# Hybrid encoder layer with a product-key expert layer: one comparison and one product for the one-hot matrices, 30 kept blocks, and weight loads tied to the rows

## Chip, core and metric

The kernel runs on one core of a Trainium2 chip. The metric is the time of one execution on the device, in microseconds (us); of several runs the median is taken. A change of the time below some 0.2% can't be told from none.

## What is computed

One layer of a hybrid encoder for 512 tokens of width 1024: attention and a recurrent unit side by side, then a product-key expert layer (PEER), then a gated input. The change lies in the expert layer, which has 16384 experts (128 x 128) of one neuron each; a token uses 16 of them for each of 8 heads, 128 in all:

```python
q = (xn @ wq).reshape(B, S, PEER_HEADS, 2, HALF_KEY)
s1 = jnp.einsum('bshd,kd->bshk', q[..., 0, :], keys1)
s2 = jnp.einsum('bshd,kd->bshk', q[..., 1, :], keys2)
v1, i1 = lax.top_k(s1, PEER_TOPK); v2, i2 = lax.top_k(s2, PEER_TOPK)
...
idx = jnp.take_along_axis(cand_idx, pos, axis=-1)      # i1 * 128 + i2 of the 16 best sums
g = jax.nn.softmax(sc, axis=-1)
...
ue = exp_u[ib]
logits = jnp.einsum('td,tkd->tk', xb, ue)
act = jax.nn.gelu(logits) * gb
ve = exp_v[ib]
out = jnp.einsum('tk,tkd->td', act, ve)
```

## The kernel before

Tokens lie in four tiles of 128. For the first three tiles the kernel does not gather experts: it multiplies all tokens with all experts and weights the result with a matrix that is zero where an expert was not chosen. For the fourth tile it gathers 128 rows of `u` and 128 rows of `v` from DRAM, one row of 1024 for each token at a time, 512 KB for each such gather (256 in all).

**First sweep**, the loop `for j in range(P)` near the end of `trunk`: 128 blocks of 128 experts. A block's row `r` (512 KB of `ut`) is loaded on SP's queue by `row_load` (line 648), split into a high part `rh` (ScalarE, line 90) and a low part `rl` (VectorE, line 92), and multiplied with the tokens in 24 matmuls of 384 columns (`u_mm`, lines 97 to 99, PSUM tile `psl`). ScalarE takes the gelu out of PSUM (line 661) into `lg`. `advance` keeps three rows ahead; `r`, `rh`, `rl` have three buffers each, `psl` two. Every split's last instruction is put in the list `pace`.

The result of a block (192 KB) is stored to DRAM (`ld<-lg`, ScalarE's queue) or, for the last KEEP = 26 blocks, kept on chip in tiles of ten blocks (`keep`), of which the third lies in a pool that `settle` opens.

Between the blocks three generators are advanced by shares; each yields a cost for each piece of work, and `Background.run(share)` advances it until the share is used:

- `top`: ranks the tokens of a tile (`topk`), tile 3 first, then 0, 1, 2. Share TOP_FIRST until tile 0 is ranked, then TOP_THEN.
- `make`: `build` for tiles 0, 1, 2. For eight tokens at a time, `hot` makes on VectorE the one-hot matrices of the two key numbers: two comparisons with a ramp (line 831) and two products of the second one with the high and the low half of the weight (line 836), each of 1024 halves; HOT_DVE = 4 sends all of them to VectorE. Sixteen small matmuls (line 856, `pg`) turn them into the weight matrix of each token, ScalarE copies it to `sg` (line 859), and every 16 tokens 1 MB goes to DRAM as `gd`. Three tiles make 48 groups of eight.
- `side`: the gathered rows of tile 3 (`rows`; line 927 for `u`, line 934 for `v`), cost 1.15 each.

When `make` is done, `settle` closes the build's pools, at block `built + REST` or when the third kept tile is due, and opens those of the second sweep. From then on the loop issues the first weights.

**Second sweep**: 128 blocks in the order that begins with block 96. `v_prep` loads `lg` (if it was not kept) and one eighth of the next chunk of weights (`weights`, line 995: 192 KB, pieces of 512 bytes, `gc<-gd`; a chunk is eight blocks, there are two buffers), multiplies them (`am`, line 1065) and splits the product into `ah` and `al`. Eighteen matmuls of 512 columns a block add up into six PSUM banks (`acc`). `side` goes on with BG_V = 1.2 a block; from block 60 on, for 16 blocks, `prepare` loads and splits the weights of the gate instead. After the last block the gathered rows that are left run beside the closing steps of the first three token tiles (`finish`); tile 3 closes last.

The program is put in order by a planner (a list scheduler with modelled costs) that may move an instruction ahead of others on its engine when its inputs are free. `add_manual_dep` gives it an order: the gathers and the rows of `side` are tied to `pace` in this way, the loads of `weights` are not. An edge of the kind Sync makes the engine wait for a semaphore.

Of the kernel before, what the change touches and what calls it, by code (L numbers as in the profile page):

```python
# [11 lines left out]
F32 = mybir.dt.float32  # L12
R = mybir.dt.float32r
BF = mybir.dt.bfloat16
HF = mybir.dt.float16
I32 = mybir.dt.int32
U32 = mybir.dt.uint32
AF = mybir.ActivationFunctionType
ALU = mybir.AluOpType
# [3 lines left out]
P = 128  # L23
# [13 lines left out]
TB = 16  # L37
GBUFS = 4

KEEP = 26  # L40
G_SCALE = 2.0 ** 14
RO_AT = [2, 1, 1, 1, 1, 1, 1, 0, 0, 1, 0, 0, 1, 0, 0, 1, 0, 0, 1, 1, 9]
TOP_FIRST, TOP_THEN, MAKE, SIDE_1, SIDE, BG_V, HOT_DVE, PREP, SIDE_2 = 2.2, 1.0, 0.5, 0.6, 1.2, 1.2, 4, 60, 2.1
MAKE_2, REST = 0.62, 3
LAST = 3
N_HOT = 13
# [14 lines left out]
def trunk(ctx, tc, x, xT, pT, pos, w_lru, w_qkv, w_out, w_q, keys, wab, w_gate, w_proj,  # L61
          vec, row, ut, u, v, out, dbg=None):
    nc = tc.nc
# [83 lines left out]
    with ExitStack() as st:  # L147
# [129 lines left out]
        for ct in range(8):  # L277
# [12 lines left out]
            if ct < 4:  # L290
# [9 lines left out]
                                     scale=col(C_CW + ct), bias=col(C_CB + ct))  # L300
# [6 lines left out]
                for da in range(4):  # L307
                    i = da * 4 + ct
# [86 lines left out]
        for blk in range(3):  # L395
            accs = []

            for t in range(NT):
                tag = ((), ("ro", "po"), ("tr", None, None, "tr"))[blk][t:t + 1]
# [28 lines left out]
            for t in range(NT):  # L428
# [5 lines left out]
                if blk == 1:  # L434
                    g = qk[:, t, :].rearrange("p (g d) -> p g d", d=64)
# [202 lines left out]
    gd = dram.tile([NTB, P, P * TB], F32, name="gd")  # L638
# [31 lines left out]
    iota2 = bp.tile([P, P, 2], HF, name="iota2")  # L670
# [133 lines left out]

    def build(t, f1, f2):

        cols = []
        for i, src in enumerate((f1, f2, qg[:, t, :])):
            pt = psb.tile([P, P], F32, tag="tr", name="ptt", bufs=2)
            nc.tensor.transpose(pt, src, ident)  # L810
            sT = bw.tile([P, P], HF, tag=f"sT{i}", name="sT", bufs=1)

            nc.scalar.activation(sT, pt, AF.Copy, scale=G_SCALE if i == 2 else 1.0)
            cols.append(sT)
        gw = bw.tile([P, 2, P], F32, tag="gw", name="gw", bufs=1)
        nc.scalar.copy(gw[:, 0, :], cols[2])
        nc.vector.scalar_tensor_tensor(gw[:, 1, :], pt, G_SCALE, gw[:, 0, :], op0=ALU.mult, op1=ALU.subtract)
        gl = bw.tile([P, P], HF, tag="gl", name="gl", bufs=1)
        nc.vector.tensor_copy(gl, gw[:, 1, :])
        cols.append(gl)  # L820

        S3 = [P, 4, P, 2]

        def along(c, t0):
            return cols[c][:, t0:t0 + 8].rearrange("p (g i) -> p g i", i=2)[:, :, None, :].to_broadcast(S3)

        def hot(t0):
            o1 = bw.tile(S3, HF, tag="o1", name="o1")
            m2 = bw.tile(S3, HF, tag="m2", name="m2")
            for c, o in enumerate((o1, m2)):  # L830
                nc.vector.tensor_tensor(o, iota2[:, None, :, :].to_broadcast(S3), along(c, t0), op=ALU.is_equal)
            o2 = []
            for part in range(2):
                o = m2 if part else bw.tile(S3, HF, tag="o2", name="o2")
                if t0 // 8 % 2 * 2 + part < HOT_DVE:
                    nc.vector.tensor_tensor(o, m2, along(2 + part, t0), op=ALU.mult)
                else:
                    for i in range(8):
                        nc.scalar.activation(o[:, i // 2, :, i % 2], m2[:, i // 2, :, i % 2], AF.Copy,
                                             scale=gw[:, part, t0 + i:t0 + i + 1])  # L840
                o2.append(o)
            return o1, o2

        o12 = hot(0)
        yield 1.0
        for t0 in range(0, P, 8):
            if t0 % TB == 0:
                sg = bw.tile([P, P, TB], F32, tag="sg", name="sg")
            o1, o2 = o12
            if t0 + 8 < P:  # L850
                o12 = hot(t0 + 8)
            for q in range(0, 8, 4):
                pg = pgp.tile([P, 4, P], F32, tag="pg", name="pg")
                for i in range(q, q + 4):
                    for part in range(2):
                        nc.tensor.matmul(pg[:, i - q, :], lhsT=o1[:, i // 2, :, i % 2], rhs=o2[part][:, i // 2, :, i % 2],  # L856
                                         start=part == 0, stop=part == 1)
                s0 = t0 % TB + q
                nc.scalar.copy(sg[:, :, s0:s0 + 4].rearrange("p j t -> p t j"), pg)  # L859
            if (t0 + 8) % TB == 0:  # L860
                nc.scalar.dma_start(gd[(t * P + t0) // TB], sg.rearrange("p j t -> p (j t)"))
            yield 1.0
# [21 lines left out]
    bw = e0.enter_context(tc.tile_pool(name="bw", bufs=2, side="right", reuse_waits="tile"))  # L884

    pace, after = [], []
# [97 lines left out]
    JC = 8  # L984
# [10 lines left out]
    def weights(c, part, vp):  # L995

        if part == 0:
            gcs.append(vp.tile([P, NTB, JC, TB], F32, tag="gc", name="gc"))
        b0, b1 = part * NTB // JC, (part + 1) * NTB // JC
        j = order[c * JC]  # L1000
        nc.sync.dma_start(gcs[-1][:, b0:b1], gd[b0:b1, :, j * TB:(j + JC) * TB].rearrange("b p (j t) -> p b j t", t=TB))

    def settle():

# [10 lines left out]
    vp, gcs, built, parts = None, [], None, list(range(JC))  # L1015
    for j in range(P):
# [7 lines left out]
        else:  # L1024
            if j == P - KEEP:
                top.run(1e9)
            i = j - (P - KEEP)
# [288 lines left out]
```

## Time and profile before

| | us |
|---|---|
| median of 3 runs (lowest, highest) | 1499.4 (1499.07, 1501.27) |
| the profiled execution, its own time | 1503.23 |
| its span, first to last instruction | 1501.4 |
| up to the first sweep | 247 |
| first sweep | 650 |
| second sweep | 541 |
| end | 64 |

The stages were cut at the first and last matmul of each sweep. Busy time is what an engine spent in instructions; matmuls overlap, so a busy TensorE need not be at its peak rate, and the spacing of the starts tells the rate. In a timeline a bracket gives the idle time before an instruction and what ended it. PE is TensorE, DVE VectorE, ACT ScalarE; SPq and ACTq are the DMA issues of SP and ScalarE.

### The profile page before, as it was taken

Reading aid. Unit: us, or ns where it says so; the run is one execution under the profiler, and the core shown is the slowest. Engines: PE = TensorE matmul, PEld = TensorE weight load, DVE = VectorE, ACT = ScalarE, POOL = GpSimd, SP = SyncE. Lnnn points to the kernel's source line nnn. Section 1 sums busy time; section 2 is a strip of 40 time slices with the busy share of each in tenths; the row PEclk is TensorE's granted clock in tenths of the full one; section 3 lists DMA queues with packets and bytes.
Section 4 is the critical chain, followed back from the end, with each engine's and each line's share of the span. In section 5 each row is a group of like instructions: output and inputs, shape, how many; then the busy total and the mean of one; then the engine's idle time right before and its main releaser. Section 6 shows DMA issues by size and latency. Waiting matters only on the chain.

```text
span 1501.4 us, 22147 instructions
## 1 busy us (share of the span) xinstructions
PE 1463.8 (97%) x7907; PEld 1291.9 (86%) x7907; DVE 1254.9 (84%) x2481; ACT 738.1 (49%) x1059; POOL 388.6 (26%) x320
## 2 busy tenths in 40 slices
PE   9999999999899999999999989999999999999996
PEld 6887678899899999999999988878887888888875
DVE  7686987789999999999978658878887478878895
ACT  7974754354555655565555423333333453333345
POOL 0000000011223373235433342232222014344450
PEclk9999999999999999999999999999999999999998
DMA  7223022156789898889989899899999789999961
GB/s 257 65 90 126 15 92 81 48 195 228 238 295 336 286 349 321 309 293 330 394 306 337 304 325 348 290 308 334 348 353 340 236 272 360 362 349 363 323 224 71
DMA packets 169199, 394.21 MB, mean 263 GB/s; under 512 B 15360, under 2 KB 90880, under 8 KB 166016
## 3 DMA queue, kind: packets, MB, share of 16 engines
q1 hardware_dynamic: 112336, 207.52, 41.1%
q0 software_dynamic: 38464, 140.00, 26.2%
q10 hardware_dynamic: 18288, 45.27, 7.8%
q8 instruction: 62, 1.02, 0.3%
q14 instruction: 49, 0.40, 0.1%
HBM read 345.41 MB, written 47.32 MB: 262 GB/s over the span
## 4 chain that ended last, share of the span: by engine, by line
PE 57%; DVE 19%; DMA 9%; issue 8%; ACT 5%; POOL 1%; SPq 0%; ACTq 0%; DVEq 0%; POOLq 0%
PE acc L99 8%; PE acc L97 8%; PE acc L98 8%; PE psl L97 6%; PE psl L99 6%; PE psl L98 6%; DVE rl L92 4%; DMA r<-in_v_dram 2%; DMA r<-in_ut_dram 2%; PE ps L97 2%; PE pg L856 2%; PE ps L99 2%; PE ps L98 2%; DVE rr L927 2%; DVE h L934 1%
## 5 line engine op out<-in xcount | busy, mean ns | idle before, releaser
L90 ACT ACTIVATE rh<-r 128x1024 fp32r<-128x1024 f32 x256 | 270.9, 1059 | 466.3 <-PE psl L98 172.2
L92 DVE TENSOR_TENSOR rl<-r,rh 128x1024 fp32r<-128x1024 f32 x256 | 312.4, 1221 | 106.9 <-ACT rh L90 105.6
L97 PE MATMUL psl<-x2h,rh 128*128 128x384 f32 x1024 | 348.1, 340 | 7.2 <-ACT keep L661 4.8
L99 PE MATMUL psl<-x2h,rl 128*128 128x384 f32 x1024 | 344.1, 336 | 3.6 <-DVE rl L92 3.6
L98 PE MATMUL psl<-x2l,rh 128*128 128x384 f32 x1024 | 343.6, 336 | 0.0
L99 PE MATMUL acc<-rh,al 128*128 128x512 f32 x768 | 299.5, 390 | 2.7 <-DVE al L92 2.7
L97 PE MATMUL acc<-rh,ah 128*128 128x512 f32 x768 | 299.2, 390 | 1.6 <-ACT ah L90 1.6
L98 PE MATMUL acc<-rl,ah 128*128 128x512 f32 x768 | 299.0, 389 | 0.7 <-DVE rl L92 0.7
L895 POOL DMA_INDIRECT rr<-in_u_dram,qidx x84 | 112.7, 1342 | 387.8 <-DVE rl L92 186.2
L97 PEld LDWEIGHTS psl<-x2h,rh 128*128 128x128 f32 x1024 | 192.9, 188 | 8.8 <-ACT keep L661 5.1
L99 PEld LDWEIGHTS psl<-x2h,rl 128*128 128x128 f32 x1024 | 192.9, 188 | 5.2 <-DVE rl L92 5.1
L98 PEld LDWEIGHTS psl<-x2l,rh 128*128 128x128 f32 x1024 | 193.2, 189 | 0.0
L895 POOL DMA_INDIRECT rr<-in_v_dram,qidxv x82 | 135.7, 1655 | 196.2 <-DVE rl L92 168.9
L99 PEld LDWEIGHTS acc<-rh,al 128*128 128x128 f32 x768 | 144.1, 188 | 35.3 <-DVE al L92 5.7
L97 PEld LDWEIGHTS acc<-rh,ah 128*128 128x128 f32 x768 | 144.2, 188 | 32.4 <-ACT ah L90 2.9
L98 PEld LDWEIGHTS acc<-rl,ah 128*128 128x128 f32 x768 | 144.1, 188 | 31.0 <-DVE rl L92 1.1
L934 DVE SCALAR_TENSOR_TENSOR h<-rr,qg,h 128x1024 f32<-128x1024 f32 x82 | 105.0, 1280 | 6.4 <-DMA rr<-in_v_dram,qidxv 6.4
L927 DVE CUSTOM_DVE_ANT_0 rr<-rr,xn 128x1024 f32<-128x1024 f32 x84 | 102.2, 1218 | 5.0 <-DMA rr<-in_u_dram,qidx 5.0
L859 ACT COPY sg<-pg 128x512 f32<-128x512 f32 x96 | 95.8, 1107 | 1.0 <-ACT sc L696 0.3
L895 POOL DMA_INDIRECT xn<-in_v_dram,qidxv x46 | 67.7, 1472 | 99.4 <-DVE rl L92 92.1
L895 POOL DMA_INDIRECT xn<-in_u_dram,qidx x44 | 61.0, 1387 | 121.7 <-DVE rl L92 103.9
L90 ACT ACTIVATE ah<-am 128x384 fp32r<-128x384 f32 x128 | 65.7, 514 | 53.1 <-PE acc L98 28.7
(342 smaller groups left out, 2274.1 us busy)
## 6 DMA issues: line engine op xcount, KB each, us to landing
r<-in_ut_dram SPq DMA_DIRECT2D x128, 512.0 KB
r<-in_v_dram SPq DMA_DIRECT2D x128, 512.0 KB
gd<-sg ACTq DMA_DIRECT2D x24, 1024.0 KB
gc<-gd SPq DMA_DIRECT2D x128, 192.0 KB
ld<-lg ACTq DMA_DIRECT2D x102, 192.0 KB
lg<-ld SPq DMA_DIRECT2D x102, 192.0 KB
w<-in_w_qkv_dram SPq DMA_DIRECT2D x12, 512.0 KB
w<-in_w_out_dram SPq DMA_DIRECT2D x8, 512.0 KB
```

The source lines that it names most:

```text
L90: nc.scalar.activation(hi, src, AF.Copy, scale=1.0 if scale is None else scale)
L92: return nc.vector.tensor_sub(lo, src, hi.bitcast(F32))
L97: nc.tensor.matmul(ps, lhsT=lh, rhs=rh, start=first, stop=False)
L98: nc.tensor.matmul(ps, lhsT=lh, rhs=rl, start=False, stop=False)
L99: nc.tensor.matmul(ps, lhsT=ll, rhs=rh, start=False, stop=last)
L856: nc.tensor.matmul(pg[:, i - q, :], lhsT=o1[:, i // 2, :, i % 2], rhs=o2[part][:, i // 2, :, i % 2], start=part == 0, stop=part == 1)
L859: nc.scalar.copy(sg[:, :, s0:s0 + 4].rearrange("p j t -> p t j"), pg)
L895: g = nc.gpsimd.indirect_dma_start(out=dst, out_offset=None, in_=table, in_offset=bass.IndirectOffsetOnAxis(ap=idx, axis=0))
L927: behind(nc.vector.tensor_tensor_reduce(rr, rr, xn[:, t, :], 1.0, 0.0, ALU.mult, ALU.add, act[:, k % 16:k % 16 + 1]))
L934: behind(nc.vector.scalar_tensor_tensor(h[:, t, :], rr, qg[:, t, k:k + 1], h[:, t, :], op0=ALU.mult, op1=ALU.add))
```

## The change

One-hot matrices: the two key numbers of a tile of tokens lie in one tile `nums_`, the two halves of the weight in one tile `wts_`, eight tokens together. `hot` makes one comparison of 2048 halves, which writes the first and the third plane of a tile `o` of three, and one product of 2048, which reads the third plane twice and writes the second and the third. The low half of the weight is written as half precision by the subtraction itself; a cast falls away. HOT_DVE and its ScalarE branch go.

Kept blocks: KEEP goes from 26 to 30, which fills the third kept tile. So the ranking must be over at block 98 and not 102, and the third kept tile, and with it `settle`, is due at block 118 and not 122.

Weights: every load of `weights` waits (Sync) for `pace[-3]`, the split of the row two behind the newest.

Shares: TOP_FIRST 2.2 to 1.9, MAKE 0.5 to 0.57, SIDE_1 (the share of `side` until tile 0 is ranked) 0.6 to 0.85.

```diff
--- before.py
+++ after.py
@@ -37,10 +37,10 @@
 TB = 16
 GBUFS = 4
 
-KEEP = 26
+KEEP = 30
 G_SCALE = 2.0 ** 14
 RO_AT = [2, 1, 1, 1, 1, 1, 1, 0, 0, 1, 0, 0, 1, 0, 0, 1, 0, 0, 1, 1, 9]
-TOP_FIRST, TOP_THEN, MAKE, SIDE_1, SIDE, BG_V, HOT_DVE, PREP, SIDE_2 = 2.2, 1.0, 0.5, 0.6, 1.2, 1.2, 4, 60, 2.1
+TOP_FIRST, TOP_THEN, MAKE, SIDE_1, SIDE, BG_V, PREP, SIDE_2 = 1.9, 1.0, 0.57, 0.85, 1.2, 1.2, 60, 2.1
 MAKE_2, REST = 0.62, 3
 LAST = 3
 N_HOT = 13
@@ -804,42 +804,35 @@
 
     def build(t, f1, f2):
 
-        cols = []
+
+        nums_ = bw.tile([P, P // 8, 2, 8], HF, tag="sT0", name="sT0", bufs=1)
+        wts_ = bw.tile([P, P // 8, 2, 8], HF, tag="sT1", name="sT1", bufs=1)
+
+        def eights(a):
+            return a.rearrange("p (a b) -> p a b", b=8)
+
         for i, src in enumerate((f1, f2, qg[:, t, :])):
             pt = psb.tile([P, P], F32, tag="tr", name="ptt", bufs=2)
             nc.tensor.transpose(pt, src, ident)
-            sT = bw.tile([P, P], HF, tag=f"sT{i}", name="sT", bufs=1)
-
-            nc.scalar.activation(sT, pt, AF.Copy, scale=G_SCALE if i == 2 else 1.0)
-            cols.append(sT)
-        gw = bw.tile([P, 2, P], F32, tag="gw", name="gw", bufs=1)
-        nc.scalar.copy(gw[:, 0, :], cols[2])
-        nc.vector.scalar_tensor_tensor(gw[:, 1, :], pt, G_SCALE, gw[:, 0, :], op0=ALU.mult, op1=ALU.subtract)
-        gl = bw.tile([P, P], HF, tag="gl", name="gl", bufs=1)
-        nc.vector.tensor_copy(gl, gw[:, 1, :])
-        cols.append(gl)
-
-        S3 = [P, 4, P, 2]
+
+            nc.scalar.activation(nums_[:, :, i, :] if i < 2 else wts_[:, :, 0, :], eights(pt), AF.Copy,
+                                 scale=G_SCALE if i == 2 else 1.0)
+        gw = bw.tile([P, P], F32, tag="gw", name="gw", bufs=1)
+        nc.scalar.copy(eights(gw), wts_[:, :, 0, :])
+        nc.vector.scalar_tensor_tensor(wts_[:, :, 1, :], eights(pt), G_SCALE, eights(gw), op0=ALU.mult, op1=ALU.subtract)
+
+        S3 = [P, 8, P, 2]
 
         def along(c, t0):
-            return cols[c][:, t0:t0 + 8].rearrange("p (g i) -> p g i", i=2)[:, :, None, :].to_broadcast(S3)
+            return c[:, t0 // 8].rearrange("p c (g i) -> p (c g) i", i=2)[:, :, None, :].to_broadcast(S3)
 
         def hot(t0):
-            o1 = bw.tile(S3, HF, tag="o1", name="o1")
-            m2 = bw.tile(S3, HF, tag="m2", name="m2")
-            for c, o in enumerate((o1, m2)):
-                nc.vector.tensor_tensor(o, iota2[:, None, :, :].to_broadcast(S3), along(c, t0), op=ALU.is_equal)
-            o2 = []
-            for part in range(2):
-                o = m2 if part else bw.tile(S3, HF, tag="o2", name="o2")
-                if t0 // 8 % 2 * 2 + part < HOT_DVE:
-                    nc.vector.tensor_tensor(o, m2, along(2 + part, t0), op=ALU.mult)
-                else:
-                    for i in range(8):
-                        nc.scalar.activation(o[:, i // 2, :, i % 2], m2[:, i // 2, :, i % 2], AF.Copy,
-                                             scale=gw[:, part, t0 + i:t0 + i + 1])
-                o2.append(o)
-            return o1, o2
+
+            o = bw.tile([P, 3, 4, P, 2], HF, tag="o", name="o")
+            five = [P, 2, 4, P, 2]
+            nc.vector.tensor_tensor(o[:, 0:3:2], iota2[:, None, None].to_broadcast(five), along(nums_, t0), op=ALU.is_equal)
+            nc.vector.tensor_tensor(o[:, 1:3], o[:, 2:3].to_broadcast(five), along(wts_, t0), op=ALU.mult)
+            return o[:, 0], (o[:, 1], o[:, 2])
 
         o12 = hot(0)
         yield 1.0
@@ -998,7 +991,10 @@
             gcs.append(vp.tile([P, NTB, JC, TB], F32, tag="gc", name="gc"))
         b0, b1 = part * NTB // JC, (part + 1) * NTB // JC
         j = order[c * JC]
-        nc.sync.dma_start(gcs[-1][:, b0:b1], gd[b0:b1, :, j * TB:(j + JC) * TB].rearrange("b p (j t) -> p b j t", t=TB))
+        ld_ = nc.sync.dma_start(gcs[-1][:, b0:b1], gd[b0:b1, :, j * TB:(j + JC) * TB].rearrange("b p (j t) -> p b j t", t=TB))
+
+        tc.add_manual_dep(ld_.ins, pace[-3].ins.name,
+                          mybir.DependencyInfo(mybir.DependencyClass.Sync, mybir.DependencyReason.DATA), reason="pace")
 
     def settle():
```

## Rows read from the trace of the kernel before

**Rows 1.** The page, part 1: busy time, share and instructions by engine.

```profile
PE 1463.8 (97%) x7907; PEld 1291.9 (86%) x7907; DVE 1254.9 (84%) x2481; ACT 738.1 (49%) x1059; POOL 388.6 (26%) x320
```

**Rows 2.** Table of stages: length, busy by engine, granted clock, DMA share, GB/s.

```profile
247.00:897.00 650.00, 638.86 (x4148) 622.12 (x4149) 578.49 (x1453) 326.65 (x439) 205.76 (x127) 0.99 0.81 284
897.00:1438.00 541.00, 535.98 (x2357) 440.35 (x2356) 432.79 (x578) 209.41 (x287) 163.16 (x131) 1.00 0.94 326
...
350.00:400.00 50.00, 46.32 (x265) 44.72 (x263) 49.62 (x196) 23.41 (x32) 7.72 (x6) 1.00 0.66 216
...
700.00:750.00 50.00, 49.73 (x339) 48.50 (x338) 46.54 (x62) 26.02 (x36) 19.06 (x14) 1.00 0.98 381
...
850.00:900.00 50.00, 45.24 (x244) 44.05 (x243) 32.73 (x41) 15.32 (x22) 22.38 (x16) 0.93 0.96 334
...
1300.00:1400.00 100.00, 100.00 (x443) 82.81 (x442) 84.52 (x116) 37.08 (x51) 42.17 (x27) 1.00 1.01 352
...
1000.00:1010.00 10.00, 8.49 (x36) 5.99 (x35) 5.43 (x8) 4.00 (x5) 1.64 (x2) 1.00 0.95 333
```

**Rows 3.** Timeline of TensorE (start, length, engine, line), second sweep.

```profile
1431.97 0.39 PE L99 MATMUL acc<-rh,al 128*128 128x512 f32 x1
1432.20 0.39 PE L97 MATMUL acc<-rh,ah 128*128 128x512 f32 x1
```

**Rows 4.** Timeline of ScalarE at the seam (idle before and its releaser in brackets).

```profile
861.30 0.47 ACT L661 ACTIVATE keep<-psl 128x384 f32<-128x384 f32 x1
...
865.46 0.47 ACT L661 ACTIVATE keep<-psl 128x384 f32<-128x384 f32 x1
...
880.38 1.06 ACT L90 ACTIVATE rh<-r 128x1024 fp32r<-128x1024 f32 x1 [9.02 <-DMA r<-in_ut_dram]
...
893.34 0.47 ACT L661 ACTIVATE keep<-psl 128x384 f32<-128x384 f32 x1
```

**Rows 5.** Timeline of SP's queue at the seam, runs of one kind merged.

```profile
845.42 1.13 SPq L1001 DMA_DIRECT2D gc<-gd  x2
...
861.46 7.95 SPq L1001 DMA_DIRECT2D gc<-gd  x5
```

**Rows 6.** Timeline of TensorE at the seam.

```profile
876.77 0.34 PE L99 MATMUL psl<-x2h,rl 128*128 128x384 f32 x1
881.87 0.69 PE L97 MATMUL psl<-x2h,rh 128*128 128x384 f32 x1 [4.76 <-ACT keep L661]
882.36 0.52 PE L98 MATMUL psl<-x2l,rh 128*128 128x384 f32 x1
882.68 0.52 PE L99 MATMUL psl<-x2h,rl 128*128 128x384 f32 x1
```

**Rows 7.** Timeline of SP's queue, second sweep.

```profile
990.57 7.77 SPq L1001 DMA_DIRECT2D gc<-gd  x4
```

**Rows 8.** Timeline of ScalarE, second sweep.

```profile
1001.81 1.06 ACT L90 ACTIVATE rh<-r 128x1024 fp32r<-128x1024 f32 x1 [5.42 <-DMA r<-in_v_dram]
```

**Rows 9.** Timeline of ScalarE, first sweep.

```profile
378.83 0.31 ACT L738 ACTIVATE qg<-qg 128x128 f32<-128x128 f32 x1 [3.55 <-DVE qg L737]
```

**Rows 10.** Timeline of VectorE at the end: first and last of 18 gathered rows.

```profile
1440.17 1.27 DVE L934 SCALAR_TENSOR_TENSOR h<-rr,qg,h 128x1024 f32<-128x1024 f32 x1
...
1470.58 1.28 DVE L934 SCALAR_TENSOR_TENSOR h<-xn,qg,h 128x1024 f32<-128x1024 f32 x1
```

**Rows 11.** Timeline of TensorE at the end.

```profile
1477.57 1.97 PE L1154 MATMUL turn<-ident,x 128*128 128x128 f32 x8 [2.99 <-DVE x L1148]
```

**Rows 12.** Comparisons of line 831: shortest/median/longest ns, first and last start.

```profile
L831 DVE TENSOR_TENSOR o<-iota,sT x48: 672/684/722, 401.4 to 830.4; 128x1024 f16<-128x1024 f16 x48
```

**Rows 13.** Timeline of VectorE, first sweep: three instructions back to back.

```profile
666.18 1.22 DVE L781 TENSOR_TENSOR xn<-xn,sp 128x2048 f16<-128x2048 f16 x1
667.31 0.68 DVE L836 TENSOR_TENSOR m<-m,gl 128x1024 f16<-128x1024 f16 x1
667.91 1.47 DVE L771 TENSOR_TENSOR xn<-xn 128x1024 f16<-128x1024 f16 x3
```

## The prediction, on record before the result

> **What bounds the kernel now.** I read the page first, then the table of stages, then the timelines of the places where TensorE was not busy. The page has TensorE busy 97% of the span [rows 1]. The table of stages [rows 2] says where the rest is: the first sweep (247 to 897 us) has 638.86 us busy of 650, the second (897 to 1438 us) 535.98 of 541. So most of the kernel runs at the matmul rate, which this change leaves alone: second-sweep matmuls start every 0.227 us [rows 3], 18 of them make a block of 4.09 us, and first-sweep blocks end every 4.16 us, 24 matmuls of 0.173 us [rows 4]. What can be won is idle or slowed time. It lies in four places.
>
> Place A, the seam between the sweeps. Up to 865.46 a block ended every 4.16 us; from there to 893.34, five blocks, it took 27.88 us instead of 20.8, so 7.1 us were lost. In between ScalarE waited 9.02 us for one row `r` from DRAM [rows 4]. SP's queue shows why: from 845.42 on it issued 16 weight loads `gc`, both chunk buffers, as fast as the queue took them, with the row loads between; five of them took 7.95 us to issue [rows 5]. TensorE started nothing from 876.77 to 881.87, and its granted clock, 1.00 elsewhere in the sweep's stages shown, is 0.93 over 850 to 900 us [rows 2]: a part of that stretch ran at the lower of its two levels (1.2 instead of 2.4 GHz), and matmuls behind the gap start 0.32 us apart instead of 0.173 [rows 6]. So some 4.8 us of the 7.1 are idle and the rest is slow clock.
>
> Place B, the second sweep. The same burst comes once in eight blocks. At 990.57 the last four of eight `gc` took 7.77 us to issue [rows 7], the next row load stood behind them, ScalarE waited 5.42 us for it [rows 8], and TensorE was busy 8.49 of the 10 us from 1000 on [rows 2]. Other idle of this sweep falls where ScalarE waits for the gate's weights, which the change does not touch.
>
> Place C, the first sweep apart from the seam. Of its 11.1 us idle some 4.8 are A, so 6.3 are left, 3.7 of them in 350 to 400 us, where VectorE is busy 49.62 of 50 us [rows 2]. ScalarE, in order, stands there behind a step of the top-k that waits 3.55 us for VectorE [rows 9], and the splits and results behind it come late.
>
> Place D, the end. The last 18 gathered rows run on VectorE after the second sweep, from 1440.17 to 1470.58 [rows 10]; TensorE waits 2.99 us for the last token tile's normed rows, at 1477.57 [rows 11].
>
> **The change part by part.** 1. Weights in step. Each `gc` load now waits for the row split two behind the newest. Behind it on SP stand the spilled-block loads `lg` and the next row load. That row load waits for the same split anyway, since `r` has three buffers; nothing that was free is held. What moves: chunk 0 goes out as two loads a block over four blocks, later chunks as one a block, instead of in bursts of eight or sixteen. A part is first used more than two blocks (8 us) after its load. A block at the seam then moves 512 KB of row, two loads of 192 KB and about one gathered row of 512 KB: 1.44 MB in 4.16 us, 347 GB/s. From 700 to 750 us the core moved 381 GB/s with TensorE busy 49.73 of 50 us [rows 2]. So I expect the 7.1 us to shrink to 1, a gain of 6.1 (bounds 3 and 7.1). In B I take back the 1.5 us idle behind the burst (bounds 0 and 2.5, the upper one if the later row waits ease as well).
>
> 2. One comparison, one product. For each group of eight tokens VectorE ran two comparisons and two products of 1024 halves, 0.684 us long, 48 of each [rows 12]; now it runs one of each with 2048. The like is the product of 2048 halves in the top-k. An instruction starts before the end recorded for its forerunner, so I count from start to start: 1.13 us for 2048 (666.18 to 667.31), 0.60 us for 1024 (667.31 to 667.91) [rows 13]. A group falls from 4 x 0.60 = 2.40 to 2 x 1.13 = 2.26 us, and 48 groups save 6.7 us of VectorE. The Trainium skill, VectorE: DVE Perf Modes, section "Side-by-side: where the cycles go for N=2048 bf16", gives every instruction some 150 cycles of fixed cost and 1224 ns to 2048 halves at two per cycle. The trace agrees on the duration (1.22 us), not on what one more instruction costs, which the starts put at 0.07 us (2 x 0.60 - 1.13). By the page's fixed cost 96 instructions saved would be an estimated 15 us, and the sum below would gain what place C still holds, some 4 us, giving 1484.
>
> The rest of the build is hidden: ScalarE writes the same three columns a tile, now strided, and has 323 of 650 us free [rows 2]; were it not hidden, nine writes of 0.3 us would be under 3 us. The comparison writes two separate planes. The trace has no operation with that pattern; its bounds are 1.13 us and, at the rate of the 32-bit splits of 1024 elements, which VectorE starts 1.13 us apart, 2 x 1.13 = 2.26 us. I take 1.13, since type, inner pair and repeat of the operands are as before.
>
> 3. Shares. I counted the costs that the generators yield against the shares. Before: token tile 3 is ranked at block 8, then 16 blocks at 0.6, 94 at 1.2, 3 at 2.1, 4 at 1.2 and 3 at 2.1 give 139.8, over 1.15 that is 122 gathered rows in the first sweep. The second takes 113 + 3, so 18 of 256 are left, the number the trace has at the end [rows 10]. After: 19 blocks at 0.85, 90 at 1.2, 4 at 1.2 and 6 at 2.1 give 141.6, so 124, and 16 are left. A row takes 1.2 us there: VectorE has 2.4 us less in D. The last turn waits for that chain, but also for ScalarE's steps, so I take 2.0 (bounds 0 and 2.4). In C two more rows eat 2.4 of the 6.7 us, and the top-k is thinner in the first 28 blocks (1.9 for 2.2). Of the 6.3 us idle I take 2.0 back (bounds -3 and 6.3: the order of the steps is made anew, and another step may come to stand in ScalarE's way; 3 is about what the wait for the top-k cost).
>
> 4. 30 blocks kept. Four stores and four loads of 192 KB go, 1.5 MB, at 326 GB/s [rows 2] 4.7 us of DMA time for which TensorE did not wait: 0. The closing of the build pools moves from block 121 to 118, so that it comes one block behind the last group, not five. The first result in the third kept tile, and the first weights, may have to wait for the last 1 MB store of `gd`. That result must leave PSUM within two blocks (8.3 us), which covers the store (3.2 us at 326 GB/s) and a queue ahead of it as long again; uncovered it costs what the idle of A cost, up to 4.8 us. I take 0.
>
> Sum: 6.1 + 1.5 + 2.0 + 2.0 = 11.6 us. The profiled execution has a span of 1501.4 us and a time of 1503.23; the median of the runs is 1499.4, so it ran 0.26% above it. The span would be 1489.8, the profiled time 1491.6, the median **1488 us**.
>
> **The rivals.** R1, the rate of the DMA engines binds, not the order. A full second-sweep block moves 512 + 192 + 192 KB and 1.04 gathered rows of 512 KB: 1.46 MB in 4.09 us, 358 GB/s. Spreading loads would then shift lateness without removing it; half of A (3.5) and D (2.0) come back: 1494. For it: even in the 10 us with the idle behind the burst the DMA share was 0.95. Against it: 1300 to 1400 us has 352 GB/s with TensorE busy 100 of 100 us, and 381 GB/s came earlier [rows 2]. The Trainium skill, DMA: Bandwidth & Descriptors, section Specifications, puts one core's share of HBM at about 358 GB/s, which would leave a full block no slack; the 381 GB/s do not bear that out as a bound.
>
> R2, the relief of VectorE pays in full: all of A (7.1), 2.5 of B, 6.3 of C and 2.4 of D return, 18.3 us: 1481. For it: VectorE is 99% full in 350 to 400 us. Against it: part of C is ScalarE's order behind top-k steps, and those remain.
>
> R3, slower: the two-plane comparison loses the rate of two per cycle. 48 x (2.26 - 1.13) = 54 us of VectorE fall on a sweep in which it is busy 578 of 650 us. If half of it shows, and A, B and D still return 9.6: 1499.4 - 9.6 + 27 = 1517. It decides once the comparison runs above some 1.5 us. Against it: operands of the same type with the same inner pair ran at 0.684 us for 1024.
>
> R4, nothing: the planner still lets weights out in a burst, for instance because the splits they wait for are early themselves, and the early closing costs what D gives: 1499.
>
> **How the numbers follow.** Forecast 0.53, R1 0.17, R2 0.17, R3 0.07, R4 0.06. About 0.2% (3 us) is what a measurement of this kernel can tell from no change. Faster: the forecast less its spoilt cases, R2 and most of R1, 0.82. Same: R4 and the weak end of R1, 0.10. Slower: R3 and a forecast spoilt by the order in C, 0.08. At best the bounds of the terms give 18.3 us (1481), at worst 3 + 0 - 3 + 0 = 0. The range reaches from just below R2 past R1 to the worst case of the terms: 1479 to 1499.
>
> **What would show it.** After the change: `gc` on SP in ones and twos between row loads; no wait of ScalarE of 5 us or more for `r` at the seam or near 1000 us; TensorE's clock at 1.00 from 850 to 900 us; 48 comparisons of about 1.22 us; 16 gathered rows after the second sweep. I am wrong if comparisons take near 2.3 us (R3), if row waits stay as long (R1, R4), or if new idle stands near the third kept tile (part 4).

## Result, and the profile of the kernel after

The changed kernel takes 1484.95 us, the median of seven runs (1482.28 to 1492.08), against 1500.8 us for the kernel before, measured beside it (seven runs, 1499.07 to 1506.64). The ratio is 0.9894, 95% interval 0.9875 to 0.9912: some 16 us, or 1.1%, faster. The forecast was 1488, the range 1479 to 1499.

The profiled execution took 1491.43 us with a span of 1489.7, so it lies 6.5 us above its own median. The same file was profiled a second time in the experiments (called `after2`: 1487.59 us, span 1485.8; median of six 1485.52). Both stand in the tables below. The page, part 1, of the kernel after, to be read against [rows 1]:

```profile
PE 1462.2 (98%) x7907; PEld 1294.2 (87%) x7907; DVE 1246.7 (84%) x2382; ACT 737.3 (49%) x1059; POOL 375.3 (25%) x320
```

VectorE has 99 instructions and 8.2 us less, TensorE the same 7907 matmuls. The table of stages of the kernel after, columns as in [rows 2]; line numbers of this kernel lie up to 7 from those of before (the gathers are line 888, the rows of `v` line 927, the loads of the weights line 994):

```profile
250.00:890.00 640.00, 634.75 (x4144) 619.88 (x4145) 571.31 (x1356) 326.42 (x438) 197.12 (x128) 1.00 0.81 284
890.00:1432.00 542.00, 538.24 (x2366) 443.50 (x2365) 434.49 (x579) 208.94 (x287) 161.41 (x132) 1.00 0.94 330
...
850.00:900.00 50.00, 49.55 (x272) 47.06 (x270) 36.66 (x50) 17.82 (x26) 28.07 (x19) 1.00 0.99 354
890.00:900.00 10.00, 9.54 (x41) 7.06 (x39) 7.36 (x13) 3.44 (x5) 4.70 (x4) 1.00 1.05 393
900.00:910.00 10.00, 7.16 (x25) 5.23 (x26) 5.63 (x11) 2.81 (x5) 2.02 (x2) 0.91 1.01 365
1000.00:1010.00 10.00, 10.00 (x46) 8.29 (x45) 8.46 (x13) 3.27 (x5) 2.43 (x3) 1.00 0.96 346
1300.00:1400.00 100.00, 100.00 (x443) 82.87 (x442) 85.39 (x118) 37.74 (x51) 44.80 (x27) 1.00 1.03 372
```

850 to 900 us, where TensorE was busy 45.24 us at a granted clock of 0.93, now has 49.55 at 1.00, and 1000 to 1010 has 10.00 for 8.49. But 900 to 910 has a hole that was not there: 7.16 us, at a clock of 0.91. In this execution the stall at the seam was moved past the seam and not removed.

The span in stages, from the first and last matmul of each sweep (us):

| | before | after | after2 |
|---|---|---|---|
| up to the first sweep (code unchanged) | 247.1 | 250.2 | 248.6 |
| first sweep | 649.2 | 639.9 | 640.8 |
| second sweep | 542.0 | 541.4 | 538.3 |
| end | 63.1 | 58.1 | 58.1 |
| span | 1501.4 | 1489.7 | 1485.8 |

The first line is no effect of the change. Up to the first sweep every engine runs the same instructions in the same order in all fourteen profiles of this document, and the stage's length goes with the time that the clock spends at its lower level in it: 6.83 us of it in before (247.1 us), 13.65 in after (250.2), 10.24 in `after2` (248.6), and 3.41 in `seam12` (below; 245.9).

The same by the places of the prediction. What a place lost is worked out from the starts of the matmuls, as the sum of what the intervals between them exceed the median interval of their kind (0.173 us in the first sweep, 0.227 in the second). A is what was lost from 860 to 930 us before, less what was lost there after; C and the rest are what the sweep gained besides.

| gain, us | forecast | after | after2 |
|---|---|---|---|
| A, the seam (7.3 lost before; 6.3 and 2.8 lost after) | 6.1 | 1.0 | 4.6 |
| B, 1000 to 1010 us (2.4 lost before, 0 after) | 1.5 | 2.4 | 2.4 |
| the gate's weights, 1130 to 1160 us (3.8 lost before; 1.0, 1.3) | 0 | 2.8 | 2.5 |
| rest of the second sweep | 0 | 1.5 | 1.4 |
| C, the first sweep without the seam | 2.0 | 2.2 | 1.3 |
| D, the end | 2.0 | 4.9 | 4.9 |
| up to the first sweep | 0 | -3.1 | -1.5 |
| sum | 11.6 | 11.7 | 15.6 |

The sum of the forecast was met in the first profile and passed in the second, its terms were not met: D is two and a half times as large as forecast, A falls short in one profile by 5.1 and in the other by 1.5, and 2.5 to 2.8 us come from a place that I had called untouched. That the first profile's sum is 11.7 is luck: these errors cancel, with 3.1 us of low clock in unchanged code among them.

**The seam after.** Four timelines of the kernel after, columns as in [rows 4 to 6]: SP's queue, ScalarE, TensorE, and GpSimd with its gathers:

```profile
892.97 0.37 SPq L994 DMA_DIRECT2D gc<-gd  x1
893.43 2.85 SPq L650 DMA_DIRECT2D r<-in_v_dram  x1
900.02 0.37 SPq L994 DMA_DIRECT2D gc<-gd  x1
```

```profile
897.68 1.06 ACT L90 ACTIVATE rh<-r 128x1024 fp32r<-128x1024 f32 x1 [5.32 <-DMA r<-in_v_dram]
...
904.69 1.06 ACT L90 ACTIVATE rh<-r 128x1024 fp32r<-128x1024 f32 x1 [5.54 <-DMA r<-in_v_dram]
```

```profile
906.21 0.50 PE L97 MATMUL acc<-rh,ah 128*128 128x512 f32 x1 [1.73 <-ACT ah L90]
...
908.44 0.63 PE L99 MATMUL acc<-rh,al 128*128 128x512 f32 x1
908.86 0.63 PE L97 MATMUL acc<-rh,ah 128*128 128x512 f32 x1
```

```profile
875.80 1.99 POOL L888 DMA_INDIRECT xn<-in_u_dram,qidx  x1 [0.30 <-issue]
878.10 1.97 POOL L888 DMA_INDIRECT xn<-in_u_dram,qidx  x1 [0.30 <-issue]
...
885.40 0.94 POOL L888 DMA_INDIRECT rr<-in_u_dram,qidx  x1 [0.30 <-issue]
886.64 0.94 POOL L888 DMA_INDIRECT xn<-in_u_dram,qidx  x1 [0.30 <-issue]
888.72 1.68 POOL L888 DMA_INDIRECT xn<-in_u_dram,qidx  x1 [1.13 <-DVE rl L92]
```

The weights go out one at a time, 0.37 us each, where five had taken 7.95 us [rows 5]; yet ScalarE waits 5.32 and 5.54 us for a row, and matmuls behind start 0.42 us apart instead of 0.227. What goes out beside the row is on GpSimd: from 875.80 on seven gathered rows of 512 KB are issued with no wait between them, and the eighth follows at 888.72, 12.9 us later. With three row loads, three weight loads and one spilled block that SP issues in the same stretch this is 6.0 MB, or 467 GB/s asked for. The table above has 393 at most, and no ten microseconds of the two sweeps moved more than 420 in any of the fourteen traces.

SP issues the row of the first wait at 885.37, 12.3 us ahead of its split; it is the transfer that is late. From issue to landing, this row in after, then the row at the same place in `seam12`, a kernel with fewer gathers there (below):

```profile
DMA to landing us min/median/max: 12.2/12.2/12.2
```

```profile
DMA to landing us min/median/max: 7.0/7.0/7.0
```

The row of the second wait, issued at 888.94, takes 15.6 us.

**The end after.** VectorE's first and last gathered row after the second sweep, and TensorE's turn of the last token tile, to be read against [rows 10, 11]:

```profile
1433.36 1.28 DVE L927 SCALAR_TENSOR_TENSOR h<-rr,qg,h 128x1024 f32<-128x1024 f32 x1
...
1460.17 1.28 DVE L927 SCALAR_TENSOR_TENSOR h<-xn,qg,h 128x1024 f32<-128x1024 f32 x1
```

```profile
1467.64 1.09 PE L1150 MATMUL turn<-ident,x 128*128 128x128 f32 x8
```

Sixteen rows are left, as counted. The last starts 28.7 us after the second sweep's last matmul; it was 32.3. TensorE reaches the turn 36.1 us after that matmul instead of 39.3, with no wait listed, where it had waited 2.99 us; the eight transposes take 1.09 us, not 1.97, and from the turn to the end it is 22.0 us for 23.8. So 3.1 us come from the earlier turn and 1.8 from a clock that no longer falls ahead of the last matmuls.

### The profile page after: what moved, and what is told of

Same layout as the page of the kernel before. It is cut to its first block, busy times and chain, and to the rows that moved or that the text cites. A ratio compares the mean times of both kernels' runs of the same rounds, so it can differ in the third digit from the quotient of the medians.

```text
span 1489.7 us, 22160 instructions
## 1 busy us (share of the span) xinstructions
PE 1462.2 (98%) x7907; PEld 1294.2 (87%) x7907; DVE 1246.7 (84%) x2382; ACT 737.3 (49%) x1059; POOL 375.3 (25%) x320
## 4 chain that ended last, share of the span: by engine, by line
PE 71%; DVE 14%; issue 5%; DMA 5%; ACT 4%; POOL 1%; SPq 0%; DVEq 0%; POOLq 0%; ACTq 0%
PE acc L99 11%; PE acc L98 11%; PE acc L97 11%; PE psl L97 7%; PE psl L99 7%; PE psl L98 7%; DVE rl L92 3%; PE pg L849 2%; PE ps L97 2%; PE ps L99 2%; PE ps L98 2%; DVE h L927 1%; DMA rr<-in_u_dram,qidx 1%; DMA r<-in_v_dram 1%; DVE rr L920 1%
## 5 line engine op out<-in xcount | busy, mean ns | idle before, releaser
L888 POOL DMA_INDIRECT rr<-in_u_dram,qidx x84 | 109.0, 1298 | 356.6 <-DVE rl L92 284.9
L888 POOL DMA_INDIRECT rr<-in_v_dram,qidxv x82 | 123.5, 1507 | 222.6 <-DVE rl L92 185.8
```

Of the source, the lines that this page charges most:

```text
L888: g = nc.gpsimd.indirect_dma_start(out=dst, out_offset=None, in_=table, in_offset=bass.IndirectOffsetOnAxis(ap=idx, axis=0))
```

## Experiments

Each ratio is against the kernel before, run on the same chip; its median lay between 1500.8 and 1501.6 us. After itself has 0.9894 [0.9875, 0.9912]. Names that begin with `u_` are the kernel after with one part undone, `a_` the kernel before with one part alone.

**The same kernel again** (no edit).

> The changed kernel once more, for a second profiled execution. Its runs lay in two groups (1482 to 1487 and 1491 to 1492 us), and the profiled one, 1491.4, lost 6.3 us in the first blocks of the second sweep, with a lower granted clock from 908 us. If the late rows there are what parts the groups: an execution of the lower group loses under 2 us there, with the clock at full level. If they belong to every execution: 5 to 7 us again, and the groups have another cause.

Measured: 1485.52 us, 0.9884 [0.9861, 0.9908]. Places that lose time move between two executions of one program (the seam 6.3 or 2.8 us, 390 to 400 us 1.1 or 4.3), so a place that only one trace shows is weak evidence.

**Weights no longer in step.**

```diff
-        tc.add_manual_dep(ld_.ins, pace[-3].ins.name, ...)
```

> The changed kernel (median 1485 us) with the weight loads set free again; the rest stays. Order theory (the bursts of weights make rows late): 16 loads stand together on SP before the second sweep and eight before every eighth block, ScalarE waits 5 us or more for rows at the seam and near 990 us, and the time rises by 6 to 12 us, to 1491 to 1497. Rate theory (the amount of DMA binds, not its order): lateness only moves, the time stays within 2 us of 1485. Relief theory (the shorter work of VectorE is the gain): within 3 us of 1485.

Measured: 1490.99 us, 0.9931 [0.9915, 0.9947], 6.0 us slower than after. SP's queue of this kernel at the seam and near 990 us, ScalarE's rows behind both bursts, and the stage behind the second:

```profile
860.13 9.52 SPq L994 DMA_DIRECT2D gc<-gd  x5
...
987.09 4.43 SPq L994 DMA_DIRECT2D gc<-gd  x4
```

```profile
880.05 1.06 ACT L90 ACTIVATE rh<-r 128x1024 fp32r<-128x1024 f32 x1 [7.26 <-DMA r<-in_ut_dram]
...
1000.79 1.06 ACT L90 ACTIVATE rh<-r 128x1024 fp32r<-128x1024 f32 x1 [3.74 <-DMA r<-in_v_dram]
```

```profile
1000.00:1010.00 10.00, 10.00 (x46) 8.29 (x45) 7.61 (x11) 4.54 (x6) 2.03 (x2) 1.00 0.96 336
```

At the seam the old picture is back, five loads in 9.52 us and a wait of 7.26 us, and 7.3 us are lost, as in before. At 987 us the burst of four is back too, but its row comes 1.7 us less late and TensorE loses nothing. So a burst is not enough for stall B: it depends on how long the burst takes. The other two kernels without the step are `a_hot` and `a_shares` (below), whose bursts of four are, in this order:

```profile
986.62 7.28 SPq L994 DMA_DIRECT2D gc<-gd  x4
```

```profile
993.12 6.59 SPq L1001 DMA_DIRECT2D gc<-gd  x4
```

With 7.77 us (before), 7.28, 6.59 and 4.43 us for the burst, 2.4, 2.3, 1.7 and 0 us are lost from 990 to 1020 us; the ten profiles of kernels with the step lose nothing there. Why the same four loads take 4.43 us in one kernel and 7.77 in another stays open. Where all of the 6.0 us lie this trace does not show: its execution (1488.13 us) was the fastest of six and lies between the two profiled ones of after.

**The step alone**, in the kernel before (the same line added).

> The kernel before with the weight loads tied to the rows, and nothing else of the change. Order theory: the seam's 7.1 us and 1.5 to 5 us of the second sweep return, 1489 to 1493. Rate theory: the lateness moves into the second sweep, within 2 us of 1501. After the run without the pace, which lost 6 us, I expect a gain of 4 to 7 us: 1494 to 1497.

Measured: 1497.97 us, 0.9969 [0.9953, 0.9985], 3.6 us gained, a little less than expected. Stall B is gone here too. The seam still loses 4.9 us between 880 and 920, though the clock stays up.

**The step one split tighter.**

```diff
-        tc.add_manual_dep(ld_.ins, pace[-3].ins.name,
+        tc.add_manual_dep(ld_.ins, pace[-2].ins.name,
```

> The changed kernel with the weight loads tied to the split one behind the newest, so that on SP the next row load is free to go before them and not after. Order theory (what stands ahead of a row in the queue makes it late): the loss in the first blocks of the second sweep falls below 2 us in every execution, 1482 to 1484. Rate theory (the bytes at the seam bind): the loss stays, 1485 to 1486.

Measured: 1497.75 us, 0.9972 [0.9956, 0.9989], 12.8 us slower than after; both theories had expected no loss. Waits of ScalarE from 1300 to 1400 us (total, times, longest) and the stage's table of this kernel:

```profile
ACT ah L90 <- DVE am L1061: 26.3, 11, 7.1
ACT rh L90 <- DMA r<-in_v_dram: 20.5, 10, 4.0
```

```profile
1300.00:1400.00 100.00, 96.37 (x407) 78.00 (x406) 79.21 (x111) 33.91 (x46) 42.55 (x26) 0.97 0.98 346
```

By the starts 8.0 us are lost in this stage. In the kernel after the first of these waits is 4.4 us and the second does not occur over the same 100 us, but in `after2` they are 13.4 us (longest 2.2) and 12.2 us (longest 3.8) with TensorE busy 100.00 of 100. So waits of this kind are absorbed up to a length, and what `pace2` adds is longer ones, 7.1 us for `ah`. The DMA engines move less here (346 for 372 GB/s), so it is not their rate. The row load stands behind the held weight load on SP: with the newer split awaited, the shortest lead of a row load over its use falls to 5.6 us in this stretch (7.5 and 6.3 in the two profiles of after). How much of the loss is the rows' and how much that of the weights and spilled blocks (`am`) the run doesn't divide. The wait costs by its distance: no loss shows with [-3], as forecast, and [-2] is dear.

**Old comparisons and products** in the kernel after (four of 1024 halves in `hot`, the four columns as before).

> The changed kernel with the old making of the one-hot matrices: two comparisons and two products of 1024 halves for each group, separate tiles, the cast. Order theory: VectorE has 6.7 us more to do in the first sweep, of which 2 show: 1487 (1485 to 1489). Relief theory: 6 us or more show: 1491 or above. Rate theory: 1485, no change.

Measured: 1491.31 us, 0.9926 [0.9911, 0.9942], 6.4 us slower.

**The new tiles, but four instructions.**

```diff
-            nc.vector.tensor_tensor(o[:, 0:3:2], ..., op=ALU.is_equal)
-            nc.vector.tensor_tensor(o[:, 1:3], ..., op=ALU.mult)
+            for k in range(2):
+                nc.vector.tensor_tensor(o[:, 2 * k], ..., one(nums_, k), op=ALU.is_equal)
+            for k in range(2):
+                nc.vector.tensor_tensor(o[:, 1 + k], o[:, 2], one(wts_, k), op=ALU.mult)
```

> The changed kernel with its tiles as they are, but the comparison and the product each in two instructions of 1024 halves again, one plane each. From start to start this is 4 x 0.60 instead of 2 x 1.135 us a group, 6.2 us of VectorE in the first sweep. If VectorE's time is what the old way cost: 1490 to 1492, as with the old making. If it was the separate tiles and their waits: 1485 to 1486.

Measured: 1490.69 us, 0.9929 [0.9912, 0.9947], 5.7 us slower. The comparisons of the kernel after and of this one (shortest/median/longest ns), and the stage 690 to 710 us of after, then of this one:

```profile
L833 DVE TENSOR_TENSOR o<-iota,sT x48: 1200/1219/1224, 417.2 to 836.6; 128x2048 f16<-128x2048 f16 x48
```

```profile
L839 DVE TENSOR_TENSOR o<-iota,sT x96: 669/684/717, 416.4 to 839.6; 128x1024 f16<-128x1024 f16 x96
```

```profile
690.00:710.00 20.00, 18.63 (x128) 18.00 (x127) 19.76 (x24) 11.17 (x13) 6.83 (x5) 1.00 0.91 321
```

```profile
690.00:710.00 20.00, 17.54 (x113) 16.78 (x112) 19.86 (x26) 9.29 (x12) 7.60 (x5) 0.91 0.87 308
```

The number of instructions carries the effect of this part; tiles, copies and column order carry none that shows. VectorE is 99% full here in both, and the kernel with 96 instructions more loses 1.1 us of TensorE's busy time and its clock there (0.91); by the starts it loses 4.6 us in this stage, where the two profiles of after lose 1.9 and 1.4. `u_nohot` has the same 17.5 us at 0.91 and loses 4.6.

**The comparisons alone**, in the kernel before.

> The kernel before with one comparison and one product, and nothing else of the change. 6.7 us of VectorE go in the first sweep. If they show as the prediction had it (2 us): 1499 to 1500. If they show as taking them away from the changed kernel did (6 us): 1494 to 1497. If the relief only pays together with the new shares: within 1 us of 1501.

Measured: 1499.27 us, 0.9993 [0.998, 1.0006]: no gain clear of the noise, and by the interval at most 3 us. The time won on VectorE is worth some 6 us with the new shares and at most half of that with the old ones. The traces agree. From the first matmul of the first sweep to the first of its block 120 (counted from 0), ahead of the seam, it takes 607.8 to 609.1 us with old shares and old comparisons (before, `a_pace`), 606.7 to 607.8 with old shares and new comparisons (`a_hot`, `u_shares`), 610.3 to 611.4 with new shares and old comparisons (`u_nohot`, `u_split4`, `a_shares`), and 605.0 to 607.7 with both new (six profiles, without `seam_even`, which has other shares ahead of the seam).

**Old shares.**

```diff
-TOP_FIRST, TOP_THEN, MAKE, SIDE_1, ... = 1.9, 1.0, 0.57, 0.85, ...
+TOP_FIRST, TOP_THEN, MAKE, SIDE_1, ... = 2.2, 1.0, 0.5, 0.6, ...
```

> The changed kernel with the shares of before (2.2, 0.5, 0.6): by the yielded costs the ranking of tile 0 ends four blocks earlier and two to four gathered rows more are left for the end. Order theory: 2.4 to 5 us more at the end and in the first 28 blocks, 1487 to 1490. If the shares carry the gain of the first sweep: 1491 or above. If they matter nowhere: within 1 us of 1485.

Measured: 1494.43 us, 0.9951 [0.9934, 0.9967], 9.5 us slower, the largest of the parts. TensorE's turn and the stage 1460 to 1480 us of this kernel:

```profile
1468.22 1.09 PE L1150 MATMUL turn<-ident,x 128*128 128x128 f32 x8 [3.00 <-DVE x L1144]
```

```profile
1460.00:1480.00 20.00, 15.02 (x62) 11.92 (x61) 11.94 (x23) 11.66 (x21) 0.00 (x0) 0.83 0.18 66
```

Eighteen rows are left again, the wait of 3 us and the lower clock (6.83 us of it) are back, and the end takes 64.1 us.

**The shares alone**, in the kernel before.

> The kernel before with the new shares (1.9, 0.57, 0.85), and nothing else of the change; by the yielded costs 17 rows instead of 18 are left for the end, and the ranking of tile 0 is thinner. By the prediction's terms (1.2 us at the end and at most 2 in the first sweep): 1498 to 1500. By what undoing them cost (9 us): 1490 to 1494. The end of the program, 63 us after the last matmul of the second sweep, should fall to 58 if the row more or less decides whether TensorE waits there long enough to lose its clock.

Measured: 1495.27 us, 0.9959 [0.994, 0.9978], 5.5 us gained; 17 rows left, the end 58.3 us. Its turn of the last token tile:

```profile
1473.68 1.09 PE L1154 MATMUL turn<-ident,x 128*128 128x128 f32 x8 [0.35 <-DVE x L1148]
```

With the other kernels the end becomes a table without an exception: with 18 rows left it took 63.1 (before), 64.1 (`u_shares`), 63.9 (`a_pace`) and 64.3 us (`a_hot`), with 16 or 17 it took 58.1 to 58.4 us in nine profiles. So it is a step and not a price for each row. With 18 rows the turn starts 39.2 us after the second sweep's last matmul, with 17 (`a_shares`, `u_keep26`) 36.6 and with 16 36.1, where it hardly waits for VectorE any more. The first row less returns all 4.9 us, the second nothing that shows.

The gate's weights divide by the shares too: the four profiles with the old shares lose 2.8 to 3.9 us between 1130 and 1160 us, the nine with the new ones (`seam12`, below, apart) 1.3 at most. GpSimd in the kernel before, then in after:

```profile
1141.43 0.59 POOL L1116 DMA_DIRECT2D w<-in_pT_dram  x1 [0.63 <-DVE act L927]
1144.68 1.04 POOL L895 DMA_INDIRECT xn<-in_u_dram,qidx  x1 [2.66 <-DVE rl L92]
1146.32 0.56 POOL L1119 DMA_DIRECT2D w<-in_w_proj_dram  x1 [0.60 <-DVE act L927]
```

```profile
1141.17 0.60 POOL L1112 DMA_DIRECT2D w<-in_pT_dram  x1
1141.80 0.55 POOL L1115 DMA_DIRECT2D w<-in_w_proj_dram  x1
```

With the old shares a gather that waits for its split stands between the first two loads of the gate, so the second goes out 4.9 us behind the first (4.1 in the other three); with the new ones it is 0.6 us in all nine.

**26 kept blocks** (`KEEP = 26`).

> The changed kernel with 26 kept blocks: four more stores and four more loads of 192 KB, the pools close at block 121 instead of 118. Order theory: the traffic is not waited for, within 1.5 us of 1485. Rate theory: 1.5 MB more at some 330 GB/s, 4.7 us, lands in stretches that are short of DMA: 1488 to 1490. If the early closing costs time, it falls below 1484.

Measured: 1486.76 us, 0.9895 [0.9876, 0.9914]: the same as after. Four spilled blocks cost nothing that can be measured, unless the later closing of the build's pools, which comes back with them, gives as much; the run does not part the two.

**Fewer gathers at the seam**, first by the share behind the build alone, then by one even share.

```diff
-... SIDE, BG_V, PREP, SIDE_2 = ... 1.2, 1.2, 60, 2.1
+... SIDE, BG_V, PREP, SIDE_2 = ... 1.2, 1.2, 60, 1.2     (seam12)
+... SIDE, BG_V, PREP, SIDE_2 = ... 1.26, 1.2, 60, 1.26   (seam_even)
```

> The changed kernel with share 1.2 in place of 2.1 for gathered rows in the last six blocks of the first sweep: 0.8 rows of 512 KB fewer for each block at the seam, and 21 instead of 16 rows left for the end. Rate theory: rows come in time, the loss at the seam (0 to 6 us) is gone, and the end grows by 5 rows of 1.2 us: 1487 to 1491. Order theory: the loss at the seam stays as it is and the end grows: 1490 to 1493. The traces tell the two apart at the seam whatever the sum.

> The changed kernel with share 1.26 for gathered rows from block 28 to the end of the first sweep, in place of 1.2 and then 2.1 in the last six blocks: by the yielded costs 124 rows in the first sweep and 16 at the end, as in the changed kernel, but 0.7 rows fewer a block at the seam. Rate theory: no loss at the seam, 1482 to 1484. If VectorE has no room for the rows earlier, the first sweep grows by what the seam gives: 1485 to 1488. Order theory: the loss at the seam stays.

Measured: `seam12` 1504.64 us, 1.0013 [1.0, 1.0027]; `seam_even` 1489.55 us, 0.9922 [0.9905, 0.994]. The stage 860 to 910 us of `seam12`; then 510 to 540 and 860 to 930 us of `seam_even`; then 510 to 540 us of after:

```profile
860.00:910.00 50.00, 50.00 (x258) 45.99 (x258) 37.37 (x54) 18.80 (x27) 22.41 (x15) 1.00 0.97 342
```

```profile
510.00:540.00 30.00, 26.49 (x181) 25.19 (x180) 30.00 (x52) 20.29 (x23) 11.11 (x6) 1.00 0.86 292
...
860.00:930.00 70.00, 70.00 (x361) 64.39 (x360) 52.76 (x71) 26.22 (x38) 30.53 (x19) 1.00 0.96 335
```

```profile
510.00:540.00 30.00, 28.73 (x196) 27.94 (x196) 30.00 (x51) 20.58 (x24) 15.54 (x7) 1.00 0.87 299
```

Both take the seam's loss away whole: TensorE is busy 50.00 of 50 and 70.00 of 70 us. From 40 us before the sweep's end to 10 us behind it they issue 15 and 14 gathers, after 19 and `after2` 20. So with the weights in step it is the gathers that make rows late at the seam; their count alone does not say how much, since `u_shares` issues 18 and loses only 1.6 us there, and `u_nohot` and `u_split4` issue 20 like `after2` (2.8 us) and lose 6.4 and 3.0. Neither kernel pays. `seam_even` puts the rows where VectorE has no room (30.00 of 30 us busy from 510 to 540, as in after, with TensorE busy 2.2 us less), and the first sweep takes 648.8 us, 8.9 more than in after. `seam12` leaves 21 rows for an end of 69.8 us, and the planner's new order brings a further loss at the gate, 12.1 us from 1200 to 1270, seen on GpSimd, on ScalarE and in the table of that stage:

```profile
1204.37 1.68 POOL L888 DMA_INDIRECT xn<-in_u_dram,qidx  x1 [72.41 <-DVE rl L92]
1208.11 1.68 POOL L888 DMA_INDIRECT xn<-in_u_dram,qidx  x1 [2.06 <-DVE rl L92]
1209.79 0.61 POOL L1112 DMA_DIRECT2D w<-in_pT_dram  x1
```

```profile
1216.20 0.63 ACT L90 ACTIVATE wg<-w 128x512 fp32r<-128x512 f32 x1 [5.65 <-DMA w<-in_pT_dram]
```

```profile
1200.00:1270.00 70.00, 62.24 (x253) 49.39 (x251) 48.94 (x64) 31.18 (x42) 25.20 (x24) 0.93 0.84 296
```

## Why the prediction was right, point by point

- **Which part gives what.** Undone one by one, the parts cost 6.0 (step), 6.4 (comparisons), 9.5 (shares) and 0 us within the measurement (kept blocks); alone they bring 3.6, 0 within the measurement (at most 3) and 5.5. The first sum, 21.9, is above the 15.9 of the whole change and the second, 9.1, below it: the parts need each other. VectorE's saved time counts once the shares put more work on VectorE (from 610.3 us or more to 607.7 or less up to block 120), and the shares pay more when that work has been made room for. My sum had one price for each part in one setting.

- **A failed in part.** The step that failed is "a block at the seam then moves ... about one gathered row". Where the share is 2.1 and a row costs 1.15, 1.8 gathered rows go with a block, and the trace has seven in 12.9 us, 2.3 a block: 467 GB/s asked for, where I had compared 347 with 381 and found room. The two late rows were issued 12.3 us and more ahead of their splits and took 12.2 and 15.6 us to land. R1, the rate binds and not the order, holds at this place: the two kernels with fewer gathers there lose nothing. It does not hold in the steady second sweep, where after moves 372 GB/s and `after2` 381 over 100 us with TensorE busy all of them. The Trainium skill, DMA: Bandwidth & Descriptors, section Specifications, gives some 358 GB/s for a core's share of HBM; the traces pass it, with 372 GB/s there and 393 in the ten microseconds in which the late row was on its way, so the measurement decides.

- **B and the order of SP** went as forecast in the kernel after: loads in ones and twos, the stall gone. The step alone removes the stall (`a_pace`), and where there is no step the stall grows with the time that the burst takes to issue, from 0 at 4.43 us to 2.4 at 7.77. What makes one burst slower than another is not shown.

- **C was right in size** (2.0 forecast; 2.2 and 1.3), but it is the rest of two opposite effects. Split into four instructions again, the kernel loses 5.7 us, about the 48 x (4 x 0.60 - 2 x 1.13) = 6.7 us that the starts gave for VectorE: with the new shares its time is paid in full, as R2 had it. With the shares alone (`a_shares`) the sweep up to block 120 is 2.3 us longer than before, with the comparisons alone (`a_hot`) 2.4 shorter. By the fixed cost of some 150 cycles an instruction in the Trainium skill, VectorE: DVE Perf Modes, section "Side-by-side: where the cycles go for N=2048 bf16", those 96 instructions would be an estimated 15 us; neither the starts nor the 5.7 us agree with that.

- **D was mis-sized, outside its bounds.** Two rows fewer were right. The step that failed is "A row takes 1.2 us there: VectorE has 2.4 us less in D." The price was read from the length of a row, when the chain of rows advances by (1470.58 - 1440.17) / 17 = 1.79 us a row [rows 10], because other steps of VectorE run in between: 3.6 us earlier for two. Of these the turn took 3.1, since with 16 rows it no longer waits for that chain. And I took nothing for the clock, although [rows 11] showed the turn at 1.97 us behind its wait: with the wait gone, the clock does not fall ahead of the last matmuls, and 1.8 us more return. The end took 4.9 us less, and `a_shares` and `u_keep26` have the same with 17 rows: the gain was a wait that ended, not two rows.

- **The gate's weights** I had set aside as untouched. No line of them is changed, but the planner orders everything anew, and the shares decide which gather stands between two loads on GpSimd.

- **Part 4 and the rivals.** Kept blocks: 0, as forecast, and no idle near the third kept tile. R3 fell: 1.22 us for the comparison, whatever its two planes. R4 fell. The result lies between the forecast and R2's 1481.

- **What stays open.** Why executions of one program lose 2.8 or 6.3 us at the seam; why the gathers bunch there, which was not tried; and why the burst of stall B takes longer to issue in some kernels than in another. None of the versions tried is faster than the changed kernel.

## What to carry to other kernels

Price a shortened chain by the distance of its links on the path, not by the length of one instruction, but only until the wait at its end is gone; then ask whether that wait had also cost the clock. Add up the bytes of each stretch with the shares that hold in that stretch, all queues together: spacing out one queue's loads only helps until another queue bursts. Relief of an engine can be worth little until something moves into the room, so test it together with the change that fills it, and undo parts as well as adding them alone.

## What the runs showed of the hardware that was not expected

- The granted clock can't be told from the length of one pause. Between 375 and 400 us TensorE waited 1.59 and 1.54 us in the kernel before and the clock stayed at 1.00; in `u_shares` it waited 1.53 and 1.53 us and the lower level held for 3.41 us from 391.1 on. In the end stage the wait of 3 us went with 6.83 us at the lower level in all four kernels with 18 rows, and from the turn to the end they took 23.8 to 25.1 us, where nine profiles with 16 or 17 rows took 21.6 to 22.2.
- The same code does not get the same clock each time: up to the first sweep, with the same instructions in the same order, the lower level held for 3.4 to 13.7 us in the fourteen profiles, and the stage took 245.9 to 250.2 us.
- A comparison that writes two planes with a third between them runs at 1.219 us for 2048 halves, the same as the product that writes two adjoining planes (1.221).
- The most that the DMA engines of this core moved in any ten microseconds of the two sweeps was 411 to 420 GB/s in all fourteen profiles. They moved 419 from 560 to 570 us of `a_shares` and 381 over 1300 to 1400 us of `after2` with TensorE busy all of the time. At the seam of after, where two row loads took 12.2 and 15.6 us to land, it was 393 (890 to 900 us).
